# A third output buffer in place of five chunk buffers, and smaller store packets in the first macro tile, in a rotation kernel bound by DMA

## The chip, the cores and the metric

The kernel runs on one core of one Trainium2 chip; the other cores are idle. The metric is the device time of one execution in microseconds (us), as the median of several runs. A profiled execution of the same kernel gives a trace; its span is about 2 us shorter than the device time.

## The reference

The function rotates a matrix by a quarter turn. It moves data and computes nothing.

```python
x = np.random.randn(8192, 8192).astype(np.float32)   # 256 MB
k = 1
def reference(x, k):
    return np.rot90(x, k)      # out[i, j] = x[j, 8191 - i]
```

All of `x` must be read and all of `out` written: 268.44 MB each way.

## The kernel before

The matrix is cut into 16 macro tiles of 1024 rows by 4096 columns. Each is read by 8 loads of 2 MB (128 rows by 4096 columns, 16 KB per partition). VectorE (DVE) copies each load into 8 "chunks" of 128 by 512 with the columns reversed. TensorE (PE) transposes 128x128 blocks into PSUM, ScalarE (ACT) copies PSUM into an output buffer, and ACT issues the store. Eight "groups" of 4 x 128 output rows make a macro tile, and each group becomes one store of 2 MB. So there are 128 loads and 128 stores of 2 MB (the very last store is issued as two of 1 MB), on two DMA queues: loads from SP's, stores from ACT's.

A group needs the same columns of all 8 loads of its macro tile, so the first group of a tile can't be finished before the tile's last load has landed. And each finished group frees 8 chunks, as many as one load needs.

```python
P = 128; R = 1024; RT = R // P; LAST = [4096]; W = 4096; CH = 512; G = 4; PW = 2
# ... whole_reads(): makes one 16 KB read of four adjoining 4 KB reads; cut ...
    a_pool = ctx.enter_context(tc.tile_pool(name="a_pool", bufs=2))   # loads
    r_pool = ctx.enter_context(tc.tile_pool(name="r_pool", bufs=68))  # chunks, 2 KB per partition
    o_pool = ctx.enter_context(tc.tile_pool(name="o_pool", bufs=2))   # outputs, 16 KB per partition
    psum_pool = ...                                                   # bufs=2, half a group each
    for r0, c0, C in tiles:
        last = (r0, c0, C) == tiles[-1]
        for t0 in range(0, RT, q):
            if loads < RT and loads % 4 >= 2:
                a = o_pool.tile([P, W], dt, tag="o")   # the first loads borrow output buffers
            else:
                a = a_pool.tile([P, W], dt, tag="a")
            # ... dma_start(out=a, in_=x[...]) on SP; 8 tensor_copy into chunks; cut ...
        for g0 in range(0, C // P, G):
            if last and g0 // G % 2 == 0:
                ot = a_pool.tile([P, W], dt, tag="a")  # the last tile also uses load buffers
            else:
                ot = o_pool.tile([P, W], dt, tag="o")
            S = PW if last and g0 + G == C // P else G
            for h in range(0, G, PW):
                ps = psum_pool.tile([P, PW, R], mybir.dt.float32)
                for w in range(PW):
                    for t in range(RT):
                        nc.tensor.transpose(ps[...], chunks[t, ...][...], ident)
                nc.scalar.copy(o[:, G - PW - h : G - h, :], ps[:])
                done = h + PW
                if done % S == 0:
                    # ... nc.scalar.dma_start(out=out[top : top + S * P, ...], in_=o[...]); cut ...
```

## Time and profile before

| | before |
|---|---|
| device time, median of 3 runs | 1271.42 us |
| profiled span | 1269.2 us |
| DMA | 537.55 MB, mean 424 GB/s; 428 to 430 in most slices |
| PE, ACT, DVE busy | 56%, 37%, 28% |
| from issue to landing | load 16.8 us, store 15.8 us |

From the page of the kernel before: busy shares, the DMA busy share and rate in 40 slices, and the chain that ended last.

```profile
span 1269.2 us, 10385 instructions
PE 708.7 (56%) x4096; PEld 668.1 (53%) x4096; DVE 355.2 (28%) x1024; ACT 467.2 (37%) x257; POOL 0.7 (0%) x6
DMA  9999999999999999999999999999999999999989
GB/s 400 415 431 429 429 428 429 430 428 429 428 429 428 430 430 428 429 429 430 428 428 420 429 429 429 429 429 427 428 422 427 426 421 430 427 427 427 428 342 382
DMA 78%; ACT 18%; DVE 1%; PE 1%; issue 1%; ACTq 0%; DVEq 0%
```

The kernel is bound by DMA. 537 MB at 430 GB/s take about 1249 us, so some 20 us of the span are not explained by the plain rate, and the dip in the last two slices is the largest piece. (The Trainium skill, "HBM Reference", section "Specifications (TRN2)", says that a core streaming alone reaches about 425 GB/s. This trace comes close, with 428 to 430 in its steady slices.)

The same dip in stretches of 2 us. After the length of the stretch stand the busy time and the instruction count of PE, of PE's weight loads, DVE, ACT and GpSimd, then the clock granted to PE, the DMA busy share and, last, the DMA rate in GB/s.

```profile
1212.00:1214.00 2.00, 0.13 (x1) 0.13 (x2) 0.00 (x0) 2.00 (x2) 0.00 (x0) 1.00 0.97 406
1214.00:1216.00 2.00, 0.85 (x7) 0.61 (x7) 0.00 (x0) 1.59 (x1) 0.00 (x0) 0.82 0.48 205
1216.00:1218.00 2.00, 0.00 (x0) 0.00 (x0) 0.00 (x0) 0.00 (x0) 0.00 (x0) 0.50 0.65 279
1218.00:1220.00 2.00, 1.43 (x7) 1.43 (x8) 1.91 (x6) 0.00 (x0) 0.00 (x0) 0.50 1.13 475
1220.00:1222.00 2.00, 2.00 (x11) 2.00 (x10) 0.86 (x3) 1.21 (x1) 0.00 (x0) 0.50 0.78 328
1222.00:1224.00 2.00, 2.00 (x20) 2.00 (x19) 0.00 (x0) 1.40 (x2) 0.00 (x0) 0.98 0.08 33
1224.00:1226.00 2.00, 1.79 (x17) 1.55 (x16) 0.00 (x0) 1.33 (x2) 0.00 (x0) 1.00 0.00 0
```

And the timeline at that place (start, duration, engine, line, operation, count; in brackets the idle time before and what ended it):

```profile
1211.95 3.63 ACT L137 COPY ot<-ps 128x2048 f32<-128x2048 f32 x2 [6.19 <-DMA out_dram<-ot]
1215.62 0.55 ACTq L145 DMA_DIRECT2D out_dram<-ot  x1
1218.09 2.77 DVE L111 COPY ar<-a 128x512 f32<-128x512 f32 x8 [7.05 <-DMA a<-in_x_dram]
1220.79 1.87 ACT L137 COPY ot<-ps 128x2048 f32<-128x2048 f32 x1 [5.20 <-PE ps L132]
1223.25 1.87 ACT L137 COPY ot<-ps 128x2048 f32<-128x2048 f32 x1 [0.60 <-PE ps L132]
1225.15 0.55 ACTq L145 DMA_DIRECT2D out_dram<-ot  x1
```

The last load lands at 1218.1. The first store of the last macro tile is issued at 1225.15, and until its data flow, DMA has only the older stores to move. They run out. I call this stretch **the hole**. To compare kernels I measure it in one way: in the 24 us from 6 us before the end of the last load's last packet to 18 us after it, the time lost is 24 us x (1 - rate / 429 GB/s). For the kernel before that packet ends at 1216.9 us and the rate is 314 GB/s, so 6.4 us are lost.

### The profile page before, as it was taken

How to read it: one execution, taken by the hardware profiler on the slowest of the kernel's cores; microseconds unless marked ns; L12 is line 12 of the kernel's file. 1: busy time of each engine (PE TensorE's matmuls, PEld its weight loads, DVE VectorE, ACT ScalarE, POOL GpSimd, SP SyncE). 2: the span in 40 equal slices, each digit the busy share in tenths (PEclk: the TensorE clock that was granted, in tenths of full speed). 3: DMA queues.
4: the chain of work that ended last, by engine and by line, in shares of the span. 5: the costliest groups of instructions: out<-in, count | busy, mean ns of one | idle time of the engine just before them, and what ended most of it. 6: DMA issues, size and time to landing. Idle time of an engine off the chain costs nothing.

```text
span 1269.2 us, 10385 instructions
## 1 busy us (share of the span) xinstructions
PE 708.7 (56%) x4096; PEld 668.1 (53%) x4096; DVE 355.2 (28%) x1024; ACT 467.2 (37%) x257; POOL 0.7 (0%) x6
## 2 busy tenths in 40 slices
PE   1465645655556555665566555564555555655564
PEld 0364545645555455554556545554555555545564
DVE  4422322232223222232223222332223322232210
ACT  0333334333433343333433333333433343333454
POOL 0000000000000000000000000000000000000000
PEclk9968687776777867767767677677676877768787
DMA  9999999999999999999999999999999999999989
GB/s 400 415 431 429 429 428 429 430 428 429 428 429 428 430 430 428 429 429 430 428 428 420 429 429 429 429 429 427 428 422 427 426 421 430 427 427 427 428 342 382
DMA packets 37057, 537.55 MB, mean 424 GB/s; under 512 B 4112, under 2 KB 4112, under 8 KB 4112
## 3 DMA queue, kind: packets, MB, share of 16 engines
q10 hardware_dynamic: 18576, 268.44, 49.8%
q1 hardware_dynamic: 18432, 268.44, 49.8%
q8 instruction: 32, 0.52, 0.2%
q14 instruction: 17, 0.14, 0.0%
HBM read 268.44 MB, written 268.44 MB: 423 GB/s over the span
## 4 chain that ended last, share of the span: by engine, by line
DMA 78%; ACT 18%; DVE 1%; PE 1%; issue 1%; ACTq 0%; DVEq 0%
DMA out_dram<-ot 72%; ACT ot L137 18%; DMA a<-in_x_dram 6%; DVE ar L111 1%; PE ps L132 1%; ACTq L145 0%; ACTq L137 0%; DVEq L111 0%
## 5 line engine op out<-in xcount | busy, mean ns | idle before, releaser
L132 PE MATMUL ps<-ident,ar 128*128 128x128 f32 x4096 | 708.7, 353 | 544.3 <-ACT ot L137 461.5
L132 PEld LDWEIGHTS ps<-ident,ar 128*128 128x128 f32 x4096 | 668.1, 188 | 584.6 <-ACT ot L137 492.4
L137 ACT COPY ot<-ps 128x2048 f32<-128x2048 f32 x256 | 465.9, 1869 | 747.0 <-DMA out_dram<-ot 724.2
L111 DVE COPY ar<-a 128x512 f32<-128x512 f32 x1024 | 355.2, 421 | 865.7 <-DMA a<-in_x_dram 731.6
L137 ACT ACT_TABLE_LOAD x1 | 1.3, 1283 | 41.1 <-DVE ar L111 41.1
masks.py:199 POOL TENSOR_SCALAR_AFFINE_SELECT ident<-ident 128x128 f32<-128x128 f32 x1 | 0.3, 292 | 0.1
masks.py:197 POOL MEMSET ident<- 128x128 f32 x1 | 0.2, 204 | 0.3 <-POOLq L164 0.3
L164 POOL MEMSET const-bfloat16-1.0<- 128x1 bf16 x1 | 0.1, 101 | 0.0
L164 POOL MEMSET const-uint8-127<- 128x1 uint8 x1 | 0.1, 101 | 0.0
L164 POOL MEMSET const-float32-0.0<- 128x1 f32 x1 | 0.1, 98 | 0.2 <-issue 0.2
L164 POOL MEMSET const-float32-1.0<- 128x1 f32 x1 | 0.1, 98 | 0.0
## 6 DMA issues: line engine op xcount, KB each, us to landing
a<-in_x_dram SPq DMA_DIRECT2D x128, 2048.0 KB, 16.8
out_dram<-ot ACTq DMA_DIRECT2D x127, 2048.0 KB, 15.8
out_dram<-ot ACTq DMA_DIRECT2D x2, 1024.0 KB, 12.6
```

The source lines that it names most:

```text
L111: nc.vector.tensor_copy(out=ar[:], in_=a[:, u, j * CH : (j + 1) * CH].rearrange("r (b m) -> r b m", m=P)[:, :, ::-1],)
L132: nc.tensor.transpose(ps[:, PW - 1 - w, t * P : (t + 1) * P], chunks[t, g * P // CH][:, g % (CH // P), :], ident,)
L137: nc.scalar.copy(o[:, G - PW - h : G - h, :], ps[:])
L164: nc = _bacc.Bacc("TRN2", target_bir_lowering=False, num_devices=1)
```

## The change

The change has two parts. It gives one more output buffer (16 KB per partition) at the price of five chunks (10 KB), so that one more store can be pending. And it splits the stores of the first macro tile in two, which makes their reads from SBUF 8 KB instead of 16 KB long. The intent, as I read it, is that the loads get the larger share of the DMA engines for a while and run ahead.

```diff
-LAST = [4096]
...
-    r_pool = ctx.enter_context(tc.tile_pool(name="r_pool", bufs=68))
-    o_pool = ctx.enter_context(tc.tile_pool(name="o_pool", bufs=2))
+    r_pool = ctx.enter_context(tc.tile_pool(name="r_pool", bufs=63))
+    o_pool = ctx.enter_context(tc.tile_pool(name="o_pool", bufs=3))
...
+        first = (r0, c0, C) == tiles[0]
...
-            if loads < RT and loads % 4 >= 2:
+            if loads < RT and loads % 5 >= 2:
...
-            S = PW if last and g0 + G == C // P else G
+            S = PW if first or (last and g0 + G == C // P) else G
```

(`LAST` is also dropped where it was used, which changes nothing. 64 chunks with three output buffers do not fit: the build stops with 47.34 KB per partition left for 48 KB.)

More of the change, by code (lines that the diff above doesn't have):

```diff
@@ L50, in macro_tiles @@
         widths = [W] * (M // W)
-        if r0 + R == N:
-            widths[-1:] = LAST
         c0 = 0
```

## The prediction

> **What bounds the kernel now.** DMA. The page's slices show the DMA engines at 9 tenths throughout and about 429 GB/s in nearly all of them. 537 MB at 430 GB/s are 1248.5 us of a span of 1269.2, so all that reordering can win is some 20 us, and part of that is fixed. PE, ACT and DVE are 56, 37 and 28% busy and wait for DMA.
>
> **Where DMA idles.** Stretches of 2 us show three places. The first 4 us (115 and 262 GB/s: 2.2 us lost). 54 to 60 us, when stores begin (295, 401, 410: 0.8 us lost). And before the last macro tile's stores: 205 and 279 GB/s at 1214 to 1218, 328, 33 and 0 at 1220 to 1226: about 6 us lost. The timeline tells why: the last load lands at 1218.1. Only then can the last tile's first group be transposed, copied (two copies of 1.87 us) and stored; that store is issued at 1225.2. With two output buffers the older stores were then nearly used up: the last was issued only at 1215.6, because its copy waited until 1211.9 for an earlier store to land.
>
> **What the change does.** Work and bytes stay. Eight more store issues on ACT (0.55 us each, ACT 37% busy) are free.
> 1. The first tile's stores become 8 KB packets against loads of 16 KB (an 8 KB packet takes 313 ns, a 16 KB one 613, in before's trace). The Trainium skill, "DMA: Bandwidth & Descriptors", section "Queues, rings and completion order", says each engine goes round-robin between queues, packet by packet. The trace agrees: both queues moved equal bytes while both had work. So in tile 0 loads should get about two thirds and run ahead until chunks run out.
> 2. Then 63 chunks hold the loads: load 8+n's last copy waits for the transposes of group n+1 (before: half of group n). Three buffers keep one more store pending. Together they let loads run two to three transfers further ahead of the stores, and afterwards equal shares keep that lead.
> 3. When the last load lands, two to three whole stores (4.9 us each alone) are then pending, 10 us or more of DMA work, against 7 to 8.5 us until the last tile's first store. The 6 us hole closes.
>
> In the steady part DVE will wait for PE instead of for loads; that costs nothing, since stores are always pending.
>
> **Sum.** Minus 6.1 us for the hole. Plus 0.8 us for 16.8 MB in 8 KB packets (2% slower per byte, of 39 us), plus 0.3 us because more stores drain without loads (421 GB/s there against 430). 1271.4 - 5.0 = 1266.4 us, 0.4% faster. Range 1263.5 to 1270.5. Faster by over 2%: 0.01; within 2%: 0.97; slower by over 2%: 0.02.
>
> **What would show it.** The last load lands some 10 to 20 us earlier; no 2 us stretch under 350 GB/s between 1190 us and the last store; in the waits DVE behind PE grows from 134 us to several hundred and DVE behind loads shrinks; stores take longer to land (15.8 to about 25 us). In the first tile loads move about twice the stores' bytes.
>
> **What would make it wrong.** The lead isn't kept (equal shares drift back), and the hole stays in part. Loads starve in the steady part because a load is issued too late after its chunk wait, and stores alone run at 421 GB/s. DMA semaphores shared by loads and stores couple the queues in the first tile, with three DMAs a period instead of two, and stall either.

## More of the kernel before

A second quantity is needed: **the lead**, the bytes that loads have moved minus the bytes that stores have moved, in units of 2 MB. I count it from the trace's records of DMA packets, which have queue, start, duration and size. It is the amount of data that is on the core at that moment. As both streams move in bursts, I give its mean over the 20 us that begin at the time named.

## The result

| | before | after |
|---|---|---|
| device time, median | 1271.33 us (4 runs) | 1269.65 us (1268.68 to 1270.0, 4 runs) |
| ratio | | 0.9985, 95% interval 0.9968 to 1.0003 |
| profiled span | 1269.2 us | 1266.9 us |
| last load landed | 1218.1 us | 1214.8 us |
| hole, lost | 6.4 us | 5.5 us |
| lead at 60, 200 and 1180 us | 9.41, 9.45, 9.51 | 10.17, 9.97, 9.60 |
| store, issue to landing | 15.8 us | 25.5 us |

Ratios in this document are the mean time of one kernel's runs over that of the other's runs of the same rounds, so they are not quite the ratios of the medians. With four runs even the 0.15% is not clear of noise.

The page of the kernel after:

```profile
span 1266.9 us, 10400 instructions
GB/s 399 422 425 425 428 429 428 430 429 429 429 429 428 429 429 429 429 429 429 429 428 429 429 429 429 428 428 429 428 429 427 424 429 428 429 428 423 429 355 383
DMA 82%; ACT 12%; PE 2%; DVE 2%; issue 1%; ACTq 0%; SPq 0%; DVEq 0%
```

The slices with the dip went only from 342 and 382 to 355 and 383. The 2 us stretches of the kernel after show the hole still there, three stretches wide:

```profile
1212.00:1214.00 2.00, 0.00 (x0) 0.00 (x0) 0.00 (x0) 0.14 (x1) 0.00 (x0) 0.50 0.70 295
1214.00:1216.00 2.00, 0.64 (x3) 0.64 (x4) 1.12 (x4) 0.00 (x0) 0.00 (x0) 0.50 1.09 459
1216.00:1218.00 2.00, 2.00 (x12) 2.00 (x11) 1.31 (x4) 0.42 (x1) 0.00 (x0) 0.50 0.98 418
1218.00:1220.00 2.00, 2.00 (x11) 2.00 (x10) 0.43 (x1) 1.44 (x1) 0.00 (x0) 0.50 0.37 156
1220.00:1222.00 2.00, 2.00 (x15) 2.00 (x14) 0.00 (x0) 1.01 (x1) 0.00 (x0) 0.69 0.14 57
1222.00:1224.00 2.00, 2.00 (x19) 1.76 (x18) 0.00 (x0) 1.33 (x2) 0.00 (x0) 1.00 0.12 49
```

The timeline of the kernel after, at the same place:

```profile
1208.51 3.63 ACT L138 COPY ot<-ps 128x2048 f32<-128x2048 f32 x2 [6.13 <-DMA out_dram<-ot]
1212.17 0.55 ACTq L146 DMA_DIRECT2D out_dram<-ot  x1
1214.88 2.44 DVE L109 COPY ar<-a 128x512 f32<-128x512 f32 x7 [7.06 <-DMA a<-in_x_dram]
1217.58 1.86 ACT L138 COPY ot<-ps 128x2048 f32<-128x2048 f32 x1 [5.43 <-PE ps L133]
1219.50 0.43 DVE L109 COPY ar<-a 128x512 f32<-128x512 f32 x1 [2.18 <-PE ps L133]
1220.99 1.87 ACT L138 COPY ot<-ps 128x2048 f32<-128x2048 f32 x1 [1.55 <-PE ps L133]
1222.89 0.55 ACTq L146 DMA_DIRECT2D out_dram<-ot  x1
```

From the last load's landing (1214.88) to the first store of the last tile there are now 8.0 us, 0.9 more than before. The copies of one load stand in two lines, seven and one: the 64th chunk of the tile has to wait until the tile's own first group has released a chunk.

The waits, before and after (engine and line, whom it waited for: total us, times, longest):

```profile
DVE ar L111 <- DMA a<-in_x_dram: 731.6, 109, 11.8
ACT ot L137 <- DMA out_dram<-ot: 724.2, 117, 7.1
DVE ar L111 <- PE ps L132: 134.1, 19, 7.1
ACT ot L137 <- PE ps L132: 21.3, 15, 6.1
```

```profile
DVE ar L109 <- DMA a<-in_x_dram: 730.4, 115, 8.3
ACT ot L138 <- DMA out_dram<-ot: 655.0, 105, 10.4
DVE ar L109 <- PE ps L133: 128.6, 56, 7.1
ACT ot L138 <- PE ps L133: 104.3, 22, 18.9
```

DVE does not wait longer for PE than before, so chunks do not hold the loads back for most of the run. What grew is the wait of ACT for PE, 21.3 to 104.3 us. Of this, 18.9 us are one wait before the first store; 70.0 us are 11 waits between 160 and 1160 us: at some macro tile boundaries the stores wait for the loads.

The lead, counted from the packet records, tells the story of the kernel after: it rose to 10.8 in the first macro tile, was 10.1 at 150 us, then fell by a little at each macro tile boundary (9.97 at 200 us, 9.91 at 300, 9.83 at 400, 9.73 at 500, 9.67 at 600), then hardly at all, and ended at 9.6. The kernel before stayed between 9.4 and 9.5 all the time. At the moment when it counts, the two leads differ by only 0.1. The packet records also show what this left to do for the stores: when the last load packet ended, the older tiles still had 1.05 stores of 2 MB to move, against 0.96 in the kernel before. The prediction counted on two to three.

### The profile page after: what moved, and what is told of

Its sections match the earlier page's. It is cut to its first block, busy times and chain, and to the rows that moved or that the text cites. A ratio compares the mean times of both kernels' runs of the same rounds, so it can differ in the third digit from the quotient of the medians.

```text
span 1266.9 us, 10400 instructions
## 1 busy us (share of the span) xinstructions
PE 717.4 (57%) x4096; PEld 676.8 (53%) x4096; DVE 359.9 (28%) x1024; ACT 466.6 (37%) x257; POOL 0.7 (0%) x6
## 4 chain that ended last, share of the span: by engine, by line
DMA 82%; ACT 12%; PE 2%; DVE 2%; issue 1%; ACTq 0%; SPq 0%; DVEq 0%
DMA out_dram<-ot 69%; DMA a<-in_x_dram 13%; ACT ot L138 12%; PE ps L133 2%; DVE ar L109 2%; ACTq L146 0%; SPq L98 0%; ACTq L138 0%; DVEq L109 0%
## 5 line engine op out<-in xcount | busy, mean ns | idle before, releaser
L133 PE MATMUL ps<-ident,ar 128*128 128x128 f32 x4096 | 717.4, 356 | 533.4 <-ACT ot L138 466.9
L133 PEld LDWEIGHTS ps<-ident,ar 128*128 128x128 f32 x4096 | 676.8, 190 | 573.7 <-ACT ot L138 497.7
L109 DVE COPY ar<-a 128x512 f32<-128x512 f32 x1024 | 359.9, 420 | 860.0 <-DMA a<-in_x_dram 730.4
L138 ACT ACT_TABLE_LOAD x1 | 1.3, 1283 | 25.5 <-DVE ar L109 25.5
## 6 DMA issues: line engine op xcount, KB each, us to landing
out_dram<-ot ACTq DMA_DIRECT2D x119, 2048.0 KB, 25.5
```

The source lines that it names most:

```text
L109: nc.vector.tensor_copy(out=ar[:], in_=a[:, u, j * CH : (j + 1) * CH].rearrange("r (b m) -> r b m", m=P)[:, :, ::-1],)
L133: nc.tensor.transpose(ps[:, PW - 1 - w, t * P : (t + 1) * P], chunks[t, g * P // CH][:, g % (CH // P), :], ident,)
```

## The experiments

Twelve kernels ran, each beside the kernel before on the same chip, five rounds each. The kernel before had medians of 1270.92, 1270.53, 1271.24 and 1271.69 us; compare by the ratios. The table sorts what follows. "Lead" is taken at 60 us and at 1180 us; "middle" is the time lost against 429 GB/s between 160 and 1160 us, counting the bytes of loads and stores alone. Lead, middle and hole come from the profiled execution alone. That execution is not always a typical one: in e5 it was the slowest of the five (1276.18 us), and in e10 it was one of the slower ones (1271.03 us). A notation such as 63/3 is chunks / output buffers.

| run | what | median us | ratio to before, 95% interval | lead 60, 1180 us | middle | hole |
|---|---|---|---|---|---|---|
| before | 68/2 | 1271.33 | | 9.41, 9.51 | 4.1 | 6.4 |
| after | 63/3, 8 KB first tile | 1269.65 | 0.9985 (0.9968 to 1.0003) | 10.17, 9.60 | 2.8 | 5.5 |
| e1 | after, 8 KB also in tile 14 | 1269.11 | 0.9992 (0.998 to 1.0005) | 9.93, 10.23 | 6.9 | 1.5 |
| e2 | before, 8 KB in tile 14 | 1270.82 | 1.0 (0.9987 to 1.0012) | 9.43, 10.55 | 4.2 | 4.5 |
| e3 | 63/3, no 8 KB | 1275.33 | 1.0037 (1.0023 to 1.0051) | 9.40, 9.27 | 7.0 | 6.5 |
| e4 | 68/2, 8 KB first tile | 1270.9 | 1.0001 (0.9989 to 1.0014) | 10.27, 10.52 | 6.4 | 3.4 |
| e5 | 64/2, 8 KB first tile | 1274.21 | 1.0023 (1.0009 to 1.0037) | 10.16, 10.43 | 6.7 | 6.7 |
| e6 | 63/2, 8 KB first tile | 1271.59 | 1.0004 (0.9991 to 1.0016) | 9.77, 9.53 | 5.9 | 4.9 |
| e7 | before, last tile in halves | 1270.95 | 1.0003 (0.999 to 1.0016) | 9.46, 7.36 | 4.5 | 3.6 |
| e8 | after, last tile in halves | 1278.0 | 1.0059 (1.0047 to 1.0072) | 10.21, 6.72 | 2.7 | 8.8 |
| e9 | after, first group by row block | 1268.47 | 0.9975 (0.9961 to 0.9989) | 10.19, 9.60 | 2.1 | 3.2 |
| e10 | before, first group by row block | 1269.55 | 0.9991 (0.9978 to 1.0004) | 9.50, 9.73 | 4.6 | 6.2 |
| e11 | e3, first group by row block | 1271.2 | 1.0001 (0.9988 to 1.0013) | 9.34, 8.98 | 4.8 | 6.4 |
| e12 | 63/2, three load buffers, no 8 KB | 1268.55 | 0.9977 (0.9963 to 0.9991) | 10.38, 10.53 | 3.2 | 5.5 |

### First call: is it the lead, the hand-over or the buffers?

My theory: the hole depends on the lead at the moment when the loads end, and the kernel after had lost its lead by then. Rivals: the hole is just the time that the hand-over takes, or the third buffer is what matters.

**e1**: the smaller packets once more, right before the end.

```diff
+        near = (r0, c0, C) == tiles[-2]
-            S = PW if first or (last and g0 + G == C // P) else G
+            S = PW if first or near or (last and g0 + G == C // P) else G
```

> The kernel after, with 8 KB stores also in the last macro tile but one (its stores run beside the last tile's loads). Lead theory: what decides the hole before the last tile's stores is the lead, loads moved minus stores moved in units of 2 MB, at the moment the loads end; the kernel after won 10.8 in the first tile but had only 9.6 at the end. Won again right before the end, the lead should be 10.3 or more when the loads end and no 2 us stretch should be under 350 GB/s: 1264 to 1266 us. Rival, hand-over latency: the hole of 5 us is the time from the last load's landing to the first store (copy, transposes, copies, issue) and no packet size changes it: 1269.6 to 1270.5 us, hole as before.

The lead rose again to 10.2 and the hole shrank to 1.5 us. The 24 us around the end of the loads before, after and in e1 (in this order, one fence each; the rate is the last column):

```profile
1210.90:1234.90 24.00, 15.93 (x122) 14.90 (x123) 2.92 (x9) 15.11 (x9) 0.00 (x0) 0.86 0.75 314
```

```profile
1208.10:1232.10 24.00, 16.82 (x117) 15.63 (x118) 2.86 (x8) 14.64 (x8) 0.00 (x0) 0.79 0.79 331
```

```profile
1207.30:1231.30 24.00, 17.78 (x125) 16.72 (x123) 3.29 (x9) 13.74 (x9) 0.00 (x0) 0.80 0.96 403
```

So the hole is not a fixed hand-over time. But the total did not follow: 1269.11 us instead of 1264 to 1266. The five runs fall into two clusters, 1268.38 to 1269.11 and 1271.8 to 1271.85, and the profile belongs to the slow cluster. It lost 6.9 us in the middle, where its program is the same as that of the kernel after, which lost 2.8 there. So the same code takes different courses in the middle of the run, several microseconds apart. That is as much as the whole effect under study.

**e2** is the kernel before with the same smaller packets in tile 14 alone.

```diff
-            S = PW if last and g0 + G == C // P else G
+            S = PW if near or (last and g0 + G == C // P) else G
```

> The kernel before (68 chunks, two output buffers) with 8 KB stores in the last tile but one and nowhere else in addition. Lead theory: the lead is data held in SBUF, and room for it is 2 a + 8.5 chunks + 2 output buffers against 2 + 7.9 + 3 after, so nearly the same; the lead rises from 9.5 to 10 or more and most of the hole closes: 1266 to 1268 us. Rival, that the third output buffer is what keeps stores pending: hole stays, 1271 to 1272 us.

The lead reached 10.55, but the hole shrank only to 4.5 us, and the time did not change. A miss for the lead theory: here, with two output buffers, a high lead was worth less. The likely reason is that the data are on the core, but as chunks, and two buffers let only two stores be queued.

**e3** is the kernel after without the small packets.

```diff
-            S = PW if first or (last and g0 + G == C // P) else G
+            S = PW if last and g0 + G == C // P else G
```

> 63 chunks and three output buffers, all stores of the first tile in one DMA with 16 KB reads. Lead theory: without unequal packets the lead stays where the start leaves it, about 9.5 as in the kernel before, hole about 6 us: 1270.5 to 1271.5 us. Rival, that three buffers give the gain by themselves: 1269 to 1270 us.

Both theories missed: it is slower than the kernel before by 0.37%. So the buffer part of the change *costs* time by itself. The lead started at 9.40 and sank to 9.11 at 1100 us. Then the stores run dry at the macro tile boundaries. The wait of ACT for PE grew to 269 us, where the kernel before has 21.3 (view of the waits, e3):

```profile
ACT ot L137 <- PE ps L132: 269.4, 43, 18.8
```

And this is one boundary, in stretches of 4 us. ACT has to wait for the tile's last load, the stores run out, and the DMA rate falls, though its busy share stays at 1:

```profile
1142.00:1146.00 4.00, 4.00 (x21) 4.00 (x20) 1.80 (x6) 1.87 (x1) 0.00 (x0) 0.50 1.00 426
1146.00:1150.00 4.00, 3.90 (x30) 3.66 (x29) 0.00 (x0) 2.28 (x2) 0.00 (x0) 0.86 0.99 393
1150.00:1154.00 4.00, 3.42 (x32) 3.14 (x31) 2.77 (x8) 3.23 (x2) 0.00 (x0) 1.00 1.02 344
1154.00:1158.00 4.00, 2.37 (x22) 2.13 (x21) 0.00 (x0) 3.04 (x2) 0.00 (x0) 1.00 1.00 418
```

In the packet records almost only load packets start from 1148 to 1153 us, and those that start in the microsecond from 1152 take 1052 ns on average instead of the usual 611. The slow ones are gathered in the second load of six of the later tiles (loads 73, 81, 97, 105, 113, 121, counted from 0). Why a load packet is slow there, when the loads at the start of the run are alone too and take 614 ns on average from 10 to 48 us, I did not find out.

**e4** is the kernel before with the small packets in the first tile: the other half of the change alone.

```diff
+        first = (r0, c0, C) == tiles[0]
-            S = PW if last and g0 + G == C // P else G
+            S = PW if first or (last and g0 + G == C // P) else G
```

> 68 chunks and two output buffers, first tile's stores with 8 KB reads. Lead theory: the first tile raises the lead to about 10 or more; with 68 chunks no load waits for its own tile's first group, so the lead leaks less than in the kernel after (steps of 0.08 at each macro tile there) and the end has 9.8 to 10.1: 1268.5 to 1270 us. Rival, that the buffers cause the gain: 1271.5 to 1272.5 us, as 8 KB packets alone only cost.

The lead was kept, as the theory said it would be with 68 chunks, and even higher: 10.5 from 100 us to the end. The hole shrank to 3.4 us. The time is that of the kernel before all the same, because 2.3 us more were lost in the middle (6.4 against 4.1). So e3 and e4 together say: the packets alone give 0, the buffers alone cost 0.37%, and both together come to a gain of 0.15% that is not clear of noise. The parts do not add up; the small packets of the first tile repair what the buffers do. (That much is clear of noise: the intervals of e3, 1.0023 to 1.0051, and of the kernel after, 0.9968 to 1.0003, do not overlap.)

### Second call: who drains the lead, and a cut last tile

The theory now: 63 chunks are one short of the 64 of a macro tile, so at each boundary a load waits, and the lead leaks there.

**e5** and **e6** are e4 with 64 and 63 chunks.

```diff
-    r_pool = ctx.enter_context(tc.tile_pool(name="r_pool", bufs=68))
+    r_pool = ctx.enter_context(tc.tile_pool(name="r_pool", bufs=64))   # e5; bufs=63 in e6
```

> Two output buffers, 8 KB stores in the first tile, 64 chunks: a whole macro tile, so no load waits for a group of its own tile. Leak theory (the kernel after loses its lead in steps at macro tile boundaries because 63 chunks are one short of a tile: the last load of a tile can't be copied whole before the tile's first group is transposed): the lead won in the first tile, 10 or so (smaller room than with 68), stays flat to within 0.1 from 200 to 1190 us, as it did with 68 chunks (10.53 throughout). Rival, that lead decays with fewer chunks whatever the number: it falls by 0.3 or more. Time 1270 to 1272 us.

> The same with 63 chunks. Leak theory: the lead falls in steps of 0.05 to 0.3 at the macro tile boundaries, every 78 us, from about 10 to 9.4 or 9.3; the hole before the last tile's stores is then 6 us, and slow load packets appear in the second load of each tile: 1272 to 1276 us. Rival: 63 and 64 differ by no more than 0.1 in lead and 0.5 us in time.

With 64 chunks the lead stays (10.36 at 200 us, 10.43 at the end). With 63 it is down to 9.6 at 150 us, but then it is flat up to the end (9.56 at 200 us, 9.53 at 1180). So one chunk does decide whether the lead of the first tile survives the first boundaries, but the slow leak of the kernel after is not there, though there are 63 chunks. The leak theory fails as a general account: 63 chunks with two output buffers do not leak after the start. And the times turned out the wrong way round: e5, with the higher lead, is slower, and its hole is 6.7 us in spite of a lead of 10.43 at 1180 us, almost that of e4 (10.52), whose hole is 3.4 us. So the lead alone does not decide the hole either. Why e5 is slower than the kernel before, by 0.23% with an interval clear of 1, stays open.

**e7** and **e8** cut the last macro tile into two of half the width, so that only four groups depend on the last load.

```diff
-LAST = [4096]
+LAST = [2048, 2048]          # e7; e8: the same lines put into the kernel after
```

> The kernel before with its last macro tile cut into two of half the width (4 loads and 4 groups each; loads of these two take 8 KB packets). Lead theory: only four groups now depend on the last load, so with the lead of 9.5, five stores are pending when the loads end instead of one, and the hole (6.1 us lost) closes to under 1.5 us; 8 KB load packets cost up to 1.5 us: 1265.5 to 1267.5 us. Rival, hand-over latency: the time from the last landing to the first store of the last tile is as long as before and leaves its hole: 1271 to 1272 us.

> The same cut in the kernel after (63 chunks, three output buffers, first tile in 8 KB stores). Lead theory: its hole (5.4 us) closes as well, 1264 to 1267 us, 0 to 1.5 us below the same cut in the kernel before, because the third buffer lets stores alone run at full rate. Rival: 1269.6 us as the kernel after.

Both were misses, and e8 a bad one. I had costed the 8 KB packets of these loads by their bytes, and forgotten that they also change the shares. Now the loads have the small packets and fall behind: the lead falls to 7.4 and 6.7 at 1180 us, and the last load packet ends 18 and 28 us later than in the kernels before and after (1235.1 against 1216.9 us, 1242.3 against 1214.1), with a hole of 3.6 and 8.8 us around it. From the first to the last 8 KB load packet of e8, 1131 to 1242 us, the loads moved 16.9 MB and the stores 27.8 MB. It is the first part of the change, run backwards. e8 also loses time before that hole: from 1200 to 1220 us it moved only 324 GB/s.

### Third call: a shorter hand-over

**e9, e10, e11** order the 32 transposes of each macro tile's first group by row block, over both of its PSUM tiles. The transposes of the first seven loads can then be done early, and only 4 are left for the last load. The first chunk is also released before the last load lands.

```diff
+            if g0 == 0:
+                for h in range(0, G, PW):
+                    pss[h] = psum_pool.tile([P, PW, R], mybir.dt.float32, name="ps")
+                for h, w, t in sorted(steps, key=lambda s: s[2]):     # t outermost
+                    nc.tensor.transpose(pss[h][...], chunks[t, ...][...], ident)
             for h in range(0, G, PW):
-                ps = psum_pool.tile([P, PW, R], mybir.dt.float32)
+                # group 0: ps = pss[h]; other groups as before
```

> The kernel after, with the transposes of each macro tile's first group ordered by row block (t outermost) over both of its PSUM tiles, the other groups as they were. This frees the first chunk long before the tile's last load lands, so with 63 chunks no load waits for its own tile's first group, and only 4 transposes instead of up to 25 stand between the last load and the first store. Leak theory: the lead no longer falls at each macro tile boundary (10.1 at 200 us in the kernel after, 9.6 at the end; here within 0.15 of its value at 200 us). Hand-over theory: the first store of the last tile is issued some 5 us after the last load has landed instead of 8.0. Both together: hole from 5.4 us lost to under 2; 1265 to 1267 us. If neither matters: 1269.6 us.

> The same order of the first groups in the kernel before (68 chunks, two buffers, lead 9.5). No leak to mend here, so this shows the shorter hand-over alone: the first store of the last tile is issued about 4.7 us after the last load's landing instead of 7.1, the hole shrinks from 6.1 to about 3.7 us; 1268 to 1269.5 us. If the hole were set by the lead or the number of buffers alone: 1271 us.

> 63 chunks and three buffers without the first tile's 8 KB stores (1275.3 us in its plain form, with slow load packets at each boundary because its lead sank to 9.3 and the stores ran dry), now with the first groups by row block. Leak theory: the sinking was the 64th chunk's wait; without it the lead stays at 9.4 or above and most of the boundary losses go: 1267 to 1271 us. Rival, that the boundary losses come from three buffers and a low lead whatever the wait: 1274 to 1276 us.

e9 is faster than the kernel before by 0.25%, with an interval clear of 1, though its 1268.47 us miss the expected 1265 to 1267. The timeline of e9 at the hand-over: the last load's chunks are copied in one run, 4 transposes follow, and the store is issued 4.6 us after the landing instead of 8.0.

```profile
1215.32 2.77 DVE L109 COPY ar<-a 128x512 f32<-128x512 f32 x8 [7.02 <-DMA a<-in_x_dram]
1215.81 0.66 PE L135 MATMUL ps<-ident,ar 128*128 128x128 f32 x4 [0.24 <-DVE ar L109]
1216.28 3.63 ACT L153 COPY ot<-ps 128x2048 f32<-128x2048 f32 x2 [4.17 <-PE ps L135]
1219.95 0.55 ACTq L161 DMA_DIRECT2D out_dram<-ot  x1
```

The hole shrank from 5.5 to 3.2 us at the same lead. So the hand-over has its share, as the rival said. But the lead leaked as before (10.02 to 9.60, now evenly and without steps), so that part of the expectation is refuted. The 64th chunk's wait made the steps, not the leak.

In e10 the hand-over did not get shorter in the profiled run: PSUM was not free until shortly before the last load, all 32 transposes came late, and the first store was issued 9.5 us after the landing (1215.63 to 1225.13). The hole stayed at 6.2. The median time, 1269.55, lies within 0.1 us of what was expected, but the profiled run took 1271.03. So this run does not tell whether the faster ones had the short hand-over.

e11 came down from e3's 1275.33 to 1271.2, at the edge of what was expected, but not because the lead was kept: it sank further, to 9.0. What changed is that the boundary costs less.

### Fourth call: the mirror

What is common to the kernels whose lead leaks (after, e3, e9, e11, and up to 1100 us also e1 and e8, at 9.37 and 9.70 there) is not 63 chunks, which e6 has too, but three output buffers beside two load buffers. My guess at the reason: a queue with three transfers to fall back on never runs empty, and so it may get a little more than half of the engines. **e12** turns this round: three load buffers, two output buffers, 63 chunks, and no small packets.

```diff
-    a_pool = ctx.enter_context(tc.tile_pool(name="a_pool", bufs=2))
-    r_pool = ctx.enter_context(tc.tile_pool(name="r_pool", bufs=68))
+    a_pool = ctx.enter_context(tc.tile_pool(name="a_pool", bufs=3))
+    r_pool = ctx.enter_context(tc.tile_pool(name="r_pool", bufs=63))
```

> Three load buffers and two output buffers with 63 chunks, all 8 KB stores of the first tile left out: the mirror of 63 chunks, two load buffers and three output buffers without them (1275.3 us, lead falling from 9.40 to 9.14). Depth theory: the queue that has three transfers to fall back on is the one that never runs empty and so gets a little more than half of the engines; with three output buffers the lead drifts down, with three load buffers it must drift up, from 9.4 at 60 us to 10 or more, with no packet size to help, and stay near what the chunks allow. Rival, that 63 chunks drain the lead: it falls again, to 9.3 or less. Time: 1268 to 1272 us by the depth theory, as the two output buffers still leave a hole of about 3.5 us; 1274 us or more by the rival.

The lead was 10.38 already at 60 us (9.4 were expected there), without any unequal packets, and then drifted *up*, to 10.53. Its mirror e3, with the third buffer on the other side and everything else alike (apart from which buffers the first loads borrow), started at 9.40 and drifted down, unevenly. So 63 chunks do not drain the lead. But the rise of 0.15 doesn't show the guess right: e10, with two buffers on each side, rose by more, from 9.50 to 9.73. What e12 has gained, it had from the start. The time is 1268.55 us, 0.23% under the kernel before, and its five runs lie within 0.4 us, the narrowest of all. The waits of e12 show what holds the loads now:

```profile
DVE ar L111 <- PE ps L132: 828.5, 125, 8.7
ACT ot L137 <- DMA out_dram<-ot: 730.5, 117, 11.4
```

This is the state that my prediction expected for the kernel after: DVE waits for PE, that is for free chunks, all the time, and the time did not suffer. The hole is still 5.5 us (about 3.5 were expected), though the lead was 10.5 at 1180 us. The likely reason, read from its waits and its buffers: DVE copies the last load only after the group before it has given back its chunks, and two output buffers queue only two stores.

e12 and e9 are the two versions that beat the kernel before with an interval clear of 1. Between them, and against the kernel after, the differences (1268.47, 1268.55, 1269.65) come from different calls and are not shown to be real. The combination of e12's buffers with e9's order was not tried.

One more count from the packet records joins these cases. It was made after all the runs, so no run was made to test it. "Left" is the number of 2 MB stores of the older tiles that were still to move when the last load packet ended; "wait" is the time from there to the issue of the last tile's first store. The stores left cover 4.9 us each (2 MB at 429 GB/s); "uncovered" is the rest of the wait.

| run | left | wait, us | uncovered, us | hole, us |
|---|---|---|---|---|
| before | 0.96 | 8.2 | 3.5 | 6.4 |
| after | 1.05 | 8.8 | 3.6 | 5.5 |
| e1 | 2.17 | 10.4 | -0.2 | 1.5 |
| e2 | 2.74 | 16.8 | 3.4 | 4.5 |
| e4 | 2.19 | 12.2 | 1.5 | 3.4 |
| e5 | 1.56 | 12.7 | 5.1 | 6.7 |
| e9 | 0.98 | 5.4 | 0.6 | 3.2 |
| e12 | 1.93 | 10.8 | 1.3 | 5.5 |

The hole is 1.0 to 3.4 us longer than the uncovered time in all kernels but e12, those not listed included. This would explain why neither the lead nor the hand-over alone decides: in e2 and e5 the lead was high, but the wait was longer too. In e12 the last of the older stores was issued only at 1217.7 us, 6.3 us after the loads had ended.

## Why the prediction was right or wrong

The predicted 1266.4 us with a range of 1263.5 to 1270.5 held the measured 1269.65, and "within 2%" was right. But of the predicted gain of 5.0 us only about 1.7 came, not clear of noise, and the main mechanism did not do what I said. That the time fell into the range is partly luck: the range ends less than 1 us below the time of the kernel before.

- **Right: the kernel is bound by DMA and the room is small.** No run moved the time by more than 0.6%.
- **Right: small packets shift the shares.** From 55 to 85 us of the kernel after, loads moved 7.9 MB and stores 4.6 MB (packet records, by the end of each packet), 1.7 to 1, and the lead rose from 9.4 to 10.8. The prediction said "about twice". e7 and e8 show the same with the sides exchanged.
- **Right: stores take longer to land** (15.8 to 25.5 us; predicted about 25).
- **Wrong, and the step that failed:** "Together they let loads run two to three transfers further ahead of the stores, and afterwards equal shares keep that lead." The lead grew by 1.4 transfers at its peak and by 0.6 at 150 us, and it was not kept: 0.1 was left at the end. The first half was mis-sized. What the core can hold, in units of 2 MB, is 2 loads, 68/8 chunks and 2 outputs before, which makes 12.5, against 2, 63/8 and 3 after, which makes 12.9. Five chunks for a buffer is a gain of 0.4. The rest had to come from the packets, and e4, with the packets alone, rose as high in the first tile as the kernel after (10.64 and 10.40 at 100 us): about one transfer, not two to three. The second half was named as a risk ("equal shares drift back") but not costed. The runs show when it happens: in all six kernels with three output buffers the lead sank after the first tile, and in none of those with two did it sink by more than 0.1 between 200 and 1100 us, whether they had 63, 64 or 68 chunks. Why it sinks is not shown.
- **Wrong: "The 6 us hole closes."** It went from 6.4 to 5.5 us. Step 3 of the prediction set two to three pending stores against 7 to 8.5 us; in the kernel after it was 1.05 stores against 8.8 us. Nearly closing it took both a high lead at the end and three output buffers (e1: 1.5 us). The high lead with two buffers left 3.4 us (e4), 4.5 (e2) and 6.7 (e5), and a shorter hand-over with three buffers and the low lead left 3.2 (e9). I had taken the lead as given and the hand-over as fixed, and the change even lengthened the hand-over, from 7.1 to 8.0 us.
- **Wrong: the last load 10 to 20 us earlier, DVE behind PE at several hundred us.** 3.3 us earlier, and 128.6 us. Both fit the lead that was not kept.
- **Not foreseen: the buffers alone cost 0.37%** (e3), by letting stores run dry at the macro tile boundaries. The small packets of the first tile pay for this, it seems by starting from a higher lead.

Where did the 2.3 us between the two profiles come from? 0.9 us from the hole and 1.3 us from the middle (2.8 lost against 4.1); the rest is spread. The first part fits the account above. The second I can't give to the change: e1, the same program up to tile 14, lost 6.9 us in the same stretch, so the course of a run varies by more than that. Why the courses differ, and why e4 loses 6.4 us in the middle with a lead that never falls, stays open. That the lead sinks with the third output buffer is seen in every kernel that has one. The reason by queue depth is only argued: nothing here watched a queue run empty engine by engine, and the rise that it forecast for e12 is no larger than that of e10.

## What to carry to other kernels

In a kernel that is bound by DMA with loads and stores on two queues, watch the data on the core (bytes loaded minus bytes stored) over time: here it sank in every kernel with a third output buffer, and what was set up at the start was gone when it was needed. When one pool is paid for with another, count the total room in transfers first; a swap adds much less than the new buffer suggests. And test the halves of a change one by one, since here one half cost time, the other did nothing, and together they came out no slower than before.

## What the Trainium skill lacked or had wrong

- "DMA: Bandwidth & Descriptors", section "Queues, rings and completion order", says that an engine goes round-robin between queues packet by packet. The runs agree as far as the shares go (the page's packet is typically a bundle of descriptors, while the records here show pieces of 8 or 16 KB). But the page does not draw the consequence, which decides here: the queue with the smaller packets gets the smaller share. With 8 KB against 16 KB, 1.7 to 1 in the first tile of the kernel after; in e8, with 8 KB on the loads' side, 16.9 MB of loads to 27.8 MB of stores.
- No page that I read says that load packets of the same size slow down when loads are almost alone on the engines in mid run: 690 ns on average in e3 (15 or more load packets under way at once, 160 to 1160 us) against 615 when 5 to 7 are, while loads alone at the start take 614. In e4 the same state shows 614, so being alone is not the whole cause.
- No page that I read treats the balance of two queues with different numbers of buffers: a lead that sinks from 9.34 at 60 us to 8.98 at 1180 us with three output buffers (e11), while it holds at 9.53 with two (e6, 9.56 at 200 us).
